# Two groups of outputs inside the recurrence, paired softmax sums, and narrow probabilities in spare blocks: a change to a two-layer hybrid decoder on one core

## The chip, the cores and the metric

The kernel runs on one core of a Trainium2 chip. The metric is the device time of one execution in microseconds (us); lower is better. In the profile, PE is the matrix engine (TensorE) and PEld its weight loads, DVE is VectorE, ACT is ScalarE, POOL is GpSimd and SP is the engine whose queue issues most transfers.

## The reference

Two layers with 512 tokens and a model width of 1024, all in float32. Each layer is a mixer and a gated feed-forward block; a last RMSNorm follows. What matters here is the mixer:

```python
p = n @ w_in                                   # n = RMSNorm(h)
# part A, RWKV-7: 8 heads x 64, per token
sa    = einsum('bhij,bhj->bhi', state, a_t)
state = state * w_t + sa[..., None] * b_t + v_t[..., None] * k_t
y_t   = einsum('bhij,bhj->bhi', state, r_t)
y     = group_norm(y) * lnx_w + lnx_b          # per head, over 64
y_a   = ((y + bonus) * gate) @ w_out_rwkv
# part B, MLA: 8 heads, causal softmax over 512 keys
s = (qn @ k_nope.T + qr @ k_pe.T) * scale;  s = where(key <= query, s, -1e30)
o = softmax(s) @ v
y_b = o @ w_out_mla
h = h + (sigmoid(gate_a) * y_a + sigmoid(gate_b) * y_b) @ w_out
```

## The kernel before

Each large product is three matmuls (`mm3`, lines 254 to 256): weights and operands are split into a high and a low part, and hi x hi, lo x hi and hi x lo are added in one accumulator of PSUM, tile `acc`. Weights stream from memory, 1024 columns at a time, through the queue of SP; ACT makes the high part (line 204) and DVE the low part (line 205).

PSUM has eight banks, and the pools fill all of them. In the second half of the mixer these are two banks `sc`, two banks held as one tile `xy`, one `pt`, one `po`, and two accumulators.

The recurrence is computed in eight chunks of 64 tokens. The loop `for c in range(8)` does, per chunk: eight matmuls of the state with `AR` (line 824), an add on DVE that makes `xs` (line 831), eight matmuls with the inverted triangle in `AM` (line 839), two copies into `Z` by DVE and ACT (line 844), eight matmuls with `BT` (line 849), and an add on DVE that makes the next state `St` (line 857), for which POOL has scaled the old one (line 856). All of these matmuls use parts of the matrix engine (64 x 64 or 128 x 64). So that PE has work while it waits for DVE and ACT, `filler(n)` puts n steps of gate projections between them; a step is one `mm3`. There are 20 steps in the list `rest`. A call of `filler` on an empty list does nothing.

The outputs of the recurrence come two chunks at a time from `chunk_out(i)`, i = 0 to 3. It takes the matmuls of `AR` with the stored states (line 879; half as many at i = 0, where chunk 0 has no state), those of `AM` with `Z` (line 889), then sums over each head on DVE (line 894, into `mu`) and a copy into `Z` by ACT (line 896). All four calls stand behind the recurrence (`outputs`), and use `xy`, of which there is one. `norms` then makes the group norms (lines 904 to 913), and `transposed` turns them (`yop`, line 919) into the operands `yops` of the product with `w_out_rwkv`.

Attention takes two heads at a time: `heads(p)`, p = 0 to 3. It projects keys and queries (three and twelve matmuls), and for each block b of 128 queries and each of the two heads hh it takes scores into an `sc` bank (line 981), scales and masks them and finds the minimum of the negated scores (line 984), exponentiates with the sum as a by-product (line 987), inverts the sum (line 988), scales (line 989), turns the blocks into `pt` (line 992) and copies them into `PT` (line 993). Sixteen matmuls per pair of heads make the output `po` (line 1000).

The program's order on PE is written by hand for the recurrence (`manual_schedule`). Everything else is ordered by a planner, which works through the program by priority in the order of the text and may put later work, such as attention, between the handwritten steps. On DVE, ACT and POOL the planner orders everything. Each engine then runs its list strictly in order.

In the profile each f32 matmul of the source outside `mm3` stands as two records, so the eight matmuls of line 849 are "x16".

Of the kernel before, what the change touches and what calls it, by code (L numbers as in the profile page):

```python
# [9 lines left out]
F32 = mybir.dt.float32  # L10
F32R = mybir.dt.float32r
I32 = mybir.dt.int32
AF = mybir.ActivationFunctionType
# [147 lines left out]
def build(ctx, tc, x, pos, wst, vecd, constd, out):  # L161
# [273 lines left out]
    def mixer(l, ops, nrm, wks):  # L435
        with ExitStack() as mx:
# [244 lines left out]
            def xyt():  # L681
                return pb.tile([128, 2, 512], F32, name="xy", tag="xy")

            with pool(name=f"ti{l}", bufs=2) as ti, tc.manual_schedule(engines={PE.engine}):
# [119 lines left out]
                parts4[6].go(2)  # L804


                St = [None]
                rest = iter([parts4[6]] * 4 + [parts4[7]] * 8 + [parts4[8]] * 8)

                def filler(n):  # L810
                    for _ in range(n):
                        part = next(rest, None)
                        if part:
                            part.go(1)

                for c in range(8):
                    i, e = divmod(c, 2)
                    xy = xyt()
                    if c:
                        for p in (0, 2, 1, 3):  # L820
                            for hh in range(2):
                                k0 = 64 * hh
                                s, ur, vr = slot(c, p)
                                PE.matmul(xy[ur:ur + 64, hh, 64 * p:64 * p + 64], AR[p][k0:k0 + 64, s, ur:ur + 64],
                                          St[c][k0:k0 + 64, p, :], start=True, stop=True, tile_position=(k0, ur))
                        filler(3)
                    us = tl.tile([128, 8, 64], F32, name="xs", bufs=1)
                    for g in range(2):
                        s, ur, vr = slot(c, 2 * g)
                        if c:  # L830
                            V.tensor_tensor(us[ur:ur + 64, 4 * g:4 * g + 4].rearrange("p (q h) i -> p q h i", h=2),
                                            xy[ur:ur + 64, :, 128 * g:128 * g + 128].rearrange("p h (q i) -> p q h i", i=64),
                                            Z[ur:ur + 64, i, e, 256 * g:256 * g + 256].rearrange("p (q h i) -> p q h i", h=2, i=64),
                                            ALU.add)
                    for hd in (0, 4, 1, 5, 2, 6, 3, 7):
                        s, ur, vr = slot(c, hd // 2)
                        g, n = divmod(hd, 4)
                        x = us[ur:ur + 64, hd, :] if c else Z[ur:ur + 64, i, e, 64 * hd:64 * hd + 64]
                        PE.matmul(xy[ur:ur + 64, g, 256 + 64 * n:320 + 64 * n], AM[ur:ur + 64, hd, s, ur:ur + 64], x,  # L839
                                  start=True, stop=True, tile_position=(ur, ur))  # L840
                    filler(2)
                    for g in range(2):
                        s, ur, vr = slot(c, 2 * g)
                        (A.copy if g else V.tensor_copy)(Z[ur:ur + 64, i, e, 256 * g:256 * g + 256], xy[ur:ur + 64, g, 256:512])
                    if c < 7:
                        for p in range(4):
                            for hh in range(2):
                                hd = 2 * p + hh
                                PE.matmul(xy[64 * hh:64 * hh + 64, 0, 64 * p:64 * p + 64], BT[p][:, slot(c, p)[0], 64 * hh:64 * hh + 64],
                                          Z[:, i, e, 64 * hd:64 * hd + 64], start=True, stop=True, tile_position=(0, 64 * hh))  # L850
                        filler(2)
                        Sn = tl.tile([128, 4, 64], F32, name="St", tag="St", bufs=7)
                        ps = xy[:, 0, 0:256].rearrange("p (q i) -> p q i", i=64)
                        if c:
                            tmp = tl.tile([128, 4, 64], F32, name="tmp", tag="tmp", bufs=1)
                            G.tensor_tensor(tmp, St[c], PC[:, c, :, None].to_broadcast([128, 4, 64]), ALU.mult)
                            V.tensor_tensor(Sn, ps, tmp, ALU.add)
                        else:
                            V.tensor_copy(Sn, ps)
                        St.append(Sn)  # L860

            with pool(name=f"tb{l}", bufs=2) as tb:
                def MT(name, tag, bufs=3):
# [1 line left out]

                qops = [split(xp, lat[i], vc(l, "q_norm", i), "xa", 8) for i in range(2)]
                kvop = split(xp, lat[2], None, "xa", 8)


                def chunk_out(i):  # L870
                    xy = xyt()
                    begun, left = set(), {(r, hh): 4 for r in (0, 64) for hh in range(2)}
                    for p in range(4):
                        for e, hh in ((0, 0), (1, 1), (0, 1), (1, 0)):
                            c = 2 * i + e
                            s, ur, vr = slot(c, p)
                            k0 = 64 * hh
                            if c:
                                PE.matmul(xy[vr:vr + 64, hh, 64 * p:64 * p + 64], AR[p][k0:k0 + 64, s, vr:vr + 64],
                                          St[c][k0:k0 + 64, p, :], start=(vr, hh) not in begun, stop=False,  # L880
                                          tile_position=(k0, vr))
                                begun.add((vr, hh))
                    for hh in range(2):
                        for p in range(4):
                            for e in range(2):
                                s, ur, vr = slot(2 * i + e, p)
                                hd = 2 * p + hh
                                left[vr, hh] -= 1
                                PE.matmul(xy[vr:vr + 64, hh, 64 * p:64 * p + 64], AM[:, hd, s, vr:vr + 64],  # L889
                                          Z[:, i, e, 64 * hd:64 * hd + 64], start=(vr, hh) not in begun,  # L890
                                          stop=left[vr, hh] == 0, tile_position=(0, vr))
                                begun.add((vr, hh))
                    mu = tb.tile([128, 16], F32, name="mu", bufs=4)
                    V.tensor_reduce(mu[:, 0:8].rearrange("p (q h) -> p h q", h=2),
                                    xy[:, :, 0:256].rearrange("p h (q i) -> p h q i", i=64), mybir.AxisListType.X, ALU.add)
                    A.copy(Z[:, i, 0, :].rearrange("p (q h i) -> p q h i", h=2, i=64),
                           xy[:, :, 0:256].rearrange("p h (q i) -> p q h i", i=64))
                    return mu


                def group_norm(i, mu):
# [28 lines left out]
                    V.tensor_tensor(bl, bl, gt, ALU.mult)  # L930
                    yops.append(split(xp, bl, None, "xa", 8))

                sums = []

                def outputs():
                    for i in range(4):
                        sums.append(chunk_out(i))

                def norms():
                    for i, gr in enumerate([group_norm(i, sums[i]) for i in range(4)]):  # L940
# [18 lines left out]
                def heads(p):  # L959
# [16 lines left out]
                    PTs = [tb.tile([128, 13, 128], F32, name="PT", tag="PT", bufs=4) for _ in range(2)]  # L976
                    for b in range(4):
                        n = 128 * (b + 1)
                        for hh in range(2):
                            sp = sc()  # L980
                            PE.matmul(sp[:, 0:n], qs[hh][:, 128 * b:128 * b + 128], ks[hh][:, 0:n], start=True, stop=True)  # L981
                            P = MT("P", "P")
                            mn = tb.tile([128, 4], F32, name="mn", bufs=4)
                            V.tensor_tensor_reduce(out=P[:, 0:n], in0=sp[:, 0:n],  # L984
                                                   in1=cst[:, C_CAUS + 512 - n:C_CAUS + 512], scale=-ATT_SCALE,
                                                   scalar=1e30, op0=ALU.add, op1=ALU.min, accum_out=mn[:, 0:1])
                            A.activation(P[:, 0:n], P[:, 0:n], AF.Exp, bias=mn[:, 0:1], scale=-1.0, accum_out=mn[:, 1:2])  # L987
                            V.reciprocal(mn[:, 2:3], mn[:, 1:2])
                            V.tensor_scalar(P[:, 0:n], P[:, 0:n], mn[:, 2:3], None, ALU.mult)
                            pt = pb.tile([128, 512], F32, name="pt", tag="pt")  # L990
                            for kb in range(b + 1):
                                PE.transpose(pt[:, 128 * kb:128 * kb + 128], P[:, 128 * kb:128 * kb + 128], ident)  # L992
                            A.copy(PTs[hh][:, b:4 * b + 1:3, :],  # L993
                                                                 pt[:, 0:n].rearrange("p (k q) -> p k q", q=128))
# [166 lines left out]
```

## Time and profile before

| | |
|---|---|
| three runs | 1543.62, 1544.17, 1545.25 us |
| median | 1544.17 us |
| the profiled execution: its own time | 1545.89 us |
| the profiled execution: span | 1544.1 us |
| granted clock of PE, mean | 0.998 |
| PE busy | 1525.8 us, 99% |
| DVE busy | 919.1 us, 60% |
| ACT busy | 648.2 us, 42% |

The span goes from the first to the last instruction; the execution's own time also has what lies around it, 1.8 us here. A row of the timeline gives the start, the time until the engine has finished, the engine, the source line, what is written and read, and how many instructions are merged into the row; in brackets stands idle time of the engine before it and what ended it. Matmuls overlap, so the distance between two starts says more than the length.

### The profile page before, as it was taken

The numbers are of one execution on the slowest core, as the hardware profiler recorded it, in microseconds if no ns is written. First come the engines' busy times: TensorE is split into PE (matmuls) and PEld (weight loads), VectorE is DVE, ScalarE is ACT, GpSimd is POOL, SyncE is SP. The second block draws the span as 40 slices with busy tenths as digits, with TensorE's granted clock in tenths as the row PEclk, the third lists the DMA queues.
The fourth block names the chain that finished last, engine by engine and source line by source line (L and its number), as shares of the span: only waits on it lengthen the run. The fifth ranks groups of instructions, "written<-read, shape, count | busy, mean of one in ns | idle before, by whom it ended". The sixth has DMA issues, their size and how long they took to land.

```text
span 1544.1 us, 22127 instructions
## 1 busy us (share of the span) xinstructions
PE 1525.8 (99%) x8860; PEld 1230.5 (80%) x8860; DVE 919.1 (60%) x1532; ACT 648.2 (42%) x986; POOL 186.9 (12%) x157
## 2 busy tenths in 40 slices
PE   8999999999999999999999999999999999999998
PEld 6887886678888888888887888766788888888887
DVE  5679886867455555533347668769664555554233
ACT  5545454744443333322235544457344333333222
POOL 0111101300211111100011121013012111111000
PEclk9999999999999999999999999999999999999999
DMA  5424322335332222233334333223352332333232
GB/s 197 136 89 136 112 82 90 97 103 164 109 97 100 97 96 96 96 110 116 116 117 131 101 110 103 77 92 102 111 163 96 96 96 96 98 100 100 98 96 82
DMA packets 57415, 166.05 MB, mean 108 GB/s; under 512 B 6624, under 2 KB 7904, under 8 KB 57312
## 3 DMA queue, kind: packets, MB, share of 16 engines
q1 hardware_dynamic: 57168, 164.64, 32.7%
q8 instruction: 69, 1.13, 0.3%
q14 instruction: 34, 0.28, 0.1%
q10 hardware_dynamic: 144, 0.00, 0.0%
HBM read 147.32 MB, written 17.30 MB: 107 GB/s over the span
## 4 chain that ended last, share of the span: by engine, by line
PE 96%; DVE 2%; issue 1%; ACT 1%; DMA 0%; POOLq 0%; DVEq 0%; ACTq 0%
PE acc L254 28%; PE acc L255 27%; PE acc L256 27%; PE sc L981 2%; PE pt L992 1%; PE po L1000 1%; PE m L616 1%; PE m L254 1%; PE m L256 1%; PE m L255 1%; PE xy L839 1%; PE xy L889 1%; PE xy L734 1%; PE m L624 1%; PE m L521 0%
## 5 line engine op out<-in xcount | busy, mean ns | idle before, releaser
L254 PE MATMUL acc<-hi,whi 128*128 128x512 f32 (+1 forms) x1886 | 741.6, 393 | 6.2 <-ACT hi L290 5.3
L256 PE MATMUL acc<-hi,wlo 128*128 128x512 f32 (+1 forms) x1886 | 735.7, 390 | 0.0
L255 PE MATMUL acc<-lo,whi 128*128 128x512 f32 (+1 forms) x1886 | 734.6, 390 | 0.0
L204 ACT CAST whi<-raw 128x1024 fp32r<-128x1024 f32 (+1 forms) x247 | 253.0, 1026 | 523.6 <-PE acc L255 447.2
L254 PEld LDWEIGHTS acc<-hi,whi 128*128 128x128 f32 x1886 | 355.3, 188 | 79.0 <-ACT hi L290 5.3
L256 PEld LDWEIGHTS acc<-hi,wlo 128*128 128x128 f32 x1886 | 355.0, 188 | 72.8 <-issue 1.0
L205 DVE TENSOR_TENSOR wlo<-raw,whi 128x1024 fp32r<-128x1024 f32 (+1 forms) x247 | 302.0, 1225 | 184.7 <-ACT whi L204 184.2
L255 PEld LDWEIGHTS acc<-lo,whi 128*128 128x128 f32 x1886 | 355.2, 188 | 70.1 <-issue 1.1
L1081 POOL TENSOR_TENSOR c<-c,rstd 128x512 f32<-128x512 f32 x44 | 58.0, 1317 | 403.6 <-ACT c L1080 403.6
L1074 DVE TENSOR_TENSOR u<-acc,rstd 128x512 f32<-128x512 f32 x44 | 30.5, 692 | 104.6 <-PE acc L256 104.4
L1083 DVE TENSOR_TENSOR c<-c,acc 128x512 f32<-128x512 f32 x44 | 30.3, 688 | 86.6 <-POOL c L1081 86.6
L1080 ACT ACTIVATE c<-c 128x512 f32<-128x512 f32 x44 | 27.8, 632 | 81.7 <-DVE c L1079 81.7
L313 POOL TENSOR_TENSOR nv<-nv,cst 128x4 f32<-128x4 f32 (+1 forms) x10 | 11.8, 1180 | 342.6 <-DVE nv L312 342.6
L349 POOL TENSOR_TENSOR nacc<-nacc,nsq 128x512 f32<-128x512 f32 x14 | 24.9, 1779 | 190.3 <-ACT nsq L348 190.3
L981 PE MATMUL sc<-K,q 128*128 128x128 f32 (+3 forms) x128 | 44.1, 444 | 0.2
L987 ACT ACTIVATE P<-P,mn 128x128 f32<-128x128 f32 (+3 forms) x64 | 35.8, 560 | 5.4 <-DVE mn L984 5.1
L1077 ACT ACTIVATE c<-u,vec 128x512 f32<-128x512 f32 x44 | 35.7, 811 | 2.8 <-DVE u L1073 2.8
L468 DVE TENSOR_TENSOR cur<-acc,rstd 128x512 f32<-128x512 f32 x26 | 17.9, 688 | 30.9 <-PE acc L256 25.1
L993 ACT COPY PT<-pt 128x128 f32<-128x128 f32 (+3 forms) x64 | 27.1, 423 | 16.6 <-PE pt L992 16.0
L1079 DVE SCALAR_TENSOR_TENSOR c<-u,vec,c 128x512 f32<-128x512 f32 x44 | 33.1, 752 | 1.5
L1078 DVE SCALAR_TENSOR_TENSOR c<-u,vec,c 128x512 f32<-128x512 f32 x44 | 32.8, 746 | 1.8 <-ACT c L1077 1.8
L992 PEld LDWEIGHTS pt<-cst,P 128*128 128x128 f32 x160 | 18.7, 140 | 15.5 <-ACT PT L993 9.7
(243 smaller groups left out, 1377.8 us busy)
## 6 DMA issues: line engine op xcount, KB each, us to landing
raw<-in_w SPq DMA_DIRECT2D x236, 512.0 KB, 3.3
gate_d<-gg SPq DMA_DIRECT2D x32, 256.0 KB, 2.1
AM<-gate_d SPq DMA_DIRECT2D x16, 256.0 KB, 4.6
gb<-gate_d SPq DMA_DIRECT2D x16, 256.0 KB, 2.8
raw<-in_w SPq DMA_DIRECT2D x8, 256.0 KB, 4.1
h<-in_x SPq DMA_DIRECT2D x8, 256.0 KB, 4.9
rgate_d<-gt SPq DMA_DIRECT2D x8, 256.0 KB, 3.1
bl_d<-rk SPq DMA_DIRECT2D x8, 256.0 KB, 4.3
```

Source lines behind the costliest of these rows:

```text
L204: A.copy(hi, r)
L205: V.tensor_tensor(lo, r, hi.bitcast(F32), ALU.subtract)
L254: PE.matmul(ps, w[0], xx[0], start=first, stop=False)
L255: PE.matmul(ps, w[0], xx[1], start=False, stop=False)
L256: PE.matmul(ps, w[1], xx[0], start=False, stop=last)
L981: PE.matmul(sp[:, 0:n], qs[hh][:, 128 * b:128 * b + 128], ks[hh][:, 0:n], start=True, stop=True)
L987: A.activation(P[:, 0:n], P[:, 0:n], AF.Exp, bias=mn[:, 0:1], scale=-1.0, accum_out=mn[:, 1:2])
L992: PE.transpose(pt[:, 128 * kb:128 * kb + 128], P[:, 128 * kb:128 * kb + 128], ident)
L1077: A.activation(cc, u[:, 2:514], AF.Identity, bias=vc(l, "conv_b", i), scale=vc(l, "conv_w", 2 * FT + i))
L1078: V.scalar_tensor_tensor(cc, u[:, 1:513], vc(l, "conv_w", FT + i), cc, ALU.mult, ALU.add)
L1079: V.scalar_tensor_tensor(cc, u[:, 0:512], vc(l, "conv_w", i), cc, ALU.mult, ALU.add)
L1081: G.tensor_tensor(cc, cc, rstd, ALU.mult)
```

## The change

Three edits, with what they bring along:

1. `chunk_out` moves in front of the recurrence and takes its two PSUM banks as an argument. The calls for i = 0 and 1 stand inside the recurrence, at the end of chunks 3 and 5, and use the two `sc` banks; the calls for 2 and 3 stay behind it, on `xy`. As the halves are now two tiles, sums and copy become two instructions each of half the width. The second `filler(2)` is not called in chunks 3 and 5.
2. In `heads`, the two heads of a block share one tile `mn`: both are exponentiated first, then one `reciprocal` inverts both sums, then each head is scaled and turned.
3. For b = 0 and 1, `P` is written into blocks 7, 10 and 11 of the pair's own `PT` tile, which nothing else uses, and no longer takes one of the three `P` buffers. In the last pair, for odd b, the two heads' turned blocks go into the two halves of an `xy` tile and not one after the other into `pt`.

```diff
+                def chunk_out(i, xy):
...
+                    mu = tl.tile([128, 16], F32, name="mu", bufs=4)
...
+                    for hh in range(2):
+                        ps = xy[hh][:, 0:256].rearrange("p (q i) -> p q i", i=64)
+                        V.tensor_reduce(mus[:, hh, :], ps, mybir.AxisListType.X, ALU.add)
+                        A.copy(Y[:, hh], ps)
+                    sums.append(mu)
...
-                        filler(2)
+                        if c not in (3, 5):
+                            filler(2)
...
                         St.append(Sn)
+                    if c in (3, 5):
+                        chunk_out(c // 2 - 1, [sc(), sc()])
...
-                def chunk_out(i):
-                    xy = xyt()
...
-                    mu = tb.tile([128, 16], F32, name="mu", bufs=4)
-                    V.tensor_reduce(mu[:, 0:8].rearrange("p (q h) -> p h q", h=2),
-                                    xy[:, :, 0:256].rearrange("p h (q i) -> p h q i", i=64), mybir.AxisListType.X, ALU.add)
-                    A.copy(Z[:, i, 0, :].rearrange("p (q h i) -> p q h i", h=2, i=64),
-                           xy[:, :, 0:256].rearrange("p h (q i) -> p q h i", i=64))
...
                 def outputs():
-                    for i in range(4):
-                        sums.append(chunk_out(i))
+                    for i in range(2, 4):
+                        xy = xyt()
+                        chunk_out(i, [xy[:, 0, :], xy[:, 1, :]])
...
                     for b in range(4):
                         n = 128 * (b + 1)
+                        xy3 = xyt() if p == 3 and b % 2 else None
+                        Ps = []
+                        mn = tb.tile([128, 8], F32, name="mn", bufs=2)
                         for hh in range(2):
...
-                            P = MT("P", "P")
-                            mn = tb.tile([128, 4], F32, name="mn", bufs=4)
+                            P = MT("P", "P") if b > 1 else \
+                                PTs[hh][:, 7 + 3 * b:8 + 4 * b, :].rearrange("p k q -> p (k q)")
...
-                            V.reciprocal(mn[:, 2:3], mn[:, 1:2])
-                            V.tensor_scalar(P[:, 0:n], P[:, 0:n], mn[:, 2:3], None, ALU.mult)
-                            pt = pb.tile([128, 512], F32, name="pt", tag="pt")
+                            Ps.append(P)
+                        V.reciprocal(mn[:, 4:6], mn[:, 2:4])
+                        for hh, P in enumerate(Ps):
+                            V.tensor_scalar(P[:, 0:n], P[:, 0:n], mn[:, 4 + hh:5 + hh], None, ALU.mult)
+                            pt = xy3[:, hh, :] if xy3 is not None else pb.tile([128, 512], F32, name="pt", tag="pt")
```

More of the change, by code (lines that the diff above doesn't have):

```diff
@@ L804, in mixer @@
                 parts4[6].go(2)
+                sums = []
+                def chunk_out(i, xy):
+                    begun, left = set(), {(r, hh): 4 for r in (0, 64) for hh in range(2)}
+                    for p in range(4):
+                        for e, hh in ((0, 0), (1, 1), (0, 1), (1, 0)):
+                            c = 2 * i + e
+                            s, ur, vr = slot(c, p)
+                            k0 = 64 * hh
+                            if c:
+                                PE.matmul(xy[hh][vr:vr + 64, 64 * p:64 * p + 64], AR[p][k0:k0 + 64, s, vr:vr + 64],
+                                          St[c][k0:k0 + 64, p, :], start=(vr, hh) not in begun, stop=False,
+                                          tile_position=(k0, vr))
+                                begun.add((vr, hh))
+                    for hh in range(2):
+                        for p in range(4):
+                            for e in range(2):
+                                s, ur, vr = slot(2 * i + e, p)
+                                hd = 2 * p + hh
+                                left[vr, hh] -= 1
+                                PE.matmul(xy[hh][vr:vr + 64, 64 * p:64 * p + 64], AM[:, hd, s, vr:vr + 64],
+                                          Z[:, i, e, 64 * hd:64 * hd + 64], start=(vr, hh) not in begun,
+                                          stop=left[vr, hh] == 0, tile_position=(0, vr))
+                                begun.add((vr, hh))
+                    mu = tl.tile([128, 16], F32, name="mu", bufs=4)
+                    mus = mu[:, 0:8].rearrange("p (q h) -> p h q", h=2)
+                    Y = Z[:, i, 0, :].rearrange("p (q h i) -> p h q i", h=2, i=64)
+                    for hh in range(2):
+                        ps = xy[hh][:, 0:256].rearrange("p (q i) -> p q i", i=64)
+                        V.tensor_reduce(mus[:, hh, :], ps, mybir.AxisListType.X, ALU.add)
+                        A.copy(Y[:, hh], ps)
+                    sums.append(mu)
                 St = [None]
@@ L867, in mixer @@
                 kvop = split(xp, lat[2], None, "xa", 8)
-                def chunk_out(i):
-                    xy = xyt()
[L872 to L892, printed above, removed]
-                    mu = tb.tile([128, 16], F32, name="mu", bufs=4)
-                    V.tensor_reduce(mu[:, 0:8].rearrange("p (q h) -> p h q", h=2),
-                                    xy[:, :, 0:256].rearrange("p h (q i) -> p h q i", i=64), mybir.AxisListType.X, ALU.add)
-                    A.copy(Z[:, i, 0, :].rearrange("p (q h i) -> p q h i", h=2, i=64),
-                           xy[:, :, 0:256].rearrange("p h (q i) -> p q h i", i=64))
-                    return mu
                 def group_norm(i, mu):
@@ L931, in yop @@
                     yops.append(split(xp, bl, None, "xa", 8))
-                sums = []
                 def outputs():
-                    for i in range(4):
-                        sums.append(chunk_out(i))
+                    for i in range(2, 4):
+                        xy = xyt()
+                        chunk_out(i, [xy[:, 0, :], xy[:, 1, :]])
                 def norms():
@@ L981, in heads @@
                             PE.matmul(sp[:, 0:n], qs[hh][:, 128 * b:128 * b + 128], ks[hh][:, 0:n], start=True, stop=True)
-                            P = MT("P", "P")
-                            mn = tb.tile([128, 4], F32, name="mn", bufs=4)
+                            P = MT("P", "P") if b > 1 else \
+                                PTs[hh][:, 7 + 3 * b:8 + 4 * b, :].rearrange("p k q -> p (k q)")
                             V.tensor_tensor_reduce(out=P[:, 0:n], in0=sp[:, 0:n],
                                                    in1=cst[:, C_CAUS + 512 - n:C_CAUS + 512], scale=-ATT_SCALE,
-                                                   scalar=1e30, op0=ALU.add, op1=ALU.min, accum_out=mn[:, 0:1])
-                            A.activation(P[:, 0:n], P[:, 0:n], AF.Exp, bias=mn[:, 0:1], scale=-1.0, accum_out=mn[:, 1:2])
-                            V.reciprocal(mn[:, 2:3], mn[:, 1:2])
-                            V.tensor_scalar(P[:, 0:n], P[:, 0:n], mn[:, 2:3], None, ALU.mult)
-                            pt = pb.tile([128, 512], F32, name="pt", tag="pt")
+                                                   scalar=1e30, op0=ALU.add, op1=ALU.min, accum_out=mn[:, hh:hh + 1])
+                            A.activation(P[:, 0:n], P[:, 0:n], AF.Exp, bias=mn[:, hh:hh + 1], scale=-1.0,
+                                         accum_out=mn[:, 2 + hh:3 + hh])
+                            Ps.append(P)
[3 more added lines that the diff above has]
+                            pt = xy3[:, hh, :] if xy3 is not None else pb.tile([128, 512], F32, name="pt", tag="pt")
                             for kb in range(b + 1):
```

## The prediction

> **What bounds the kernel now.** I read the page first: the share of each engine and the chain that ended last.
>
> ```profile
> PE 1525.8 (99%) x8860; PEld 1230.5 (80%) x8860; DVE 919.1 (60%) x1532; ACT 648.2 (42%) x986; POOL 186.9 (12%) x157
> PE 96%; DVE 2%; issue 1%; ACT 1%; DMA 0%; POOLq 0%; DVEq 0%; ACTq 0%
> ```
>
> PE is busy for 1525.8 of 1544.1 us and is 96% of the chain, so 18.3 us is all that better filling can bring in the whole kernel. The change removes no matmul. Next come the waits of PE, longest first (who waited for whom, total, times, longest).
>
> ```profile
> PE acc L254 <- ACT hi L290: 5.3, 1, 5.3
> PE xy L824 <- DVE St L857: 1.3, 2, 0.6
> PE xy L839 <- DVE xs L831: 1.1, 2, 0.6
> PE acc L254 <- ACT whi L204: 0.9, 1, 0.9
> PE m L624 <- DVE AM L619: 0.8, 2, 0.4
> PE m L559 <- ACT sq L555: 0.7, 1, 0.7
> PE xy L889 <- issue: 0.4, 1, 0.4
> PE xy L919 <- DVE bl L927: 0.2, 1, 0.2
> ```
>
> The first is the start of the kernel, the fourth stands between the layers, and L624 and L559 come before the recurrence: the change reaches none of these. It reaches L824 and L839 (the recurrence, once in each layer), L889 and L919: 3.0 us in all. Then the timeline of PE, to see where in the recurrence the two waits lie (layer 0; layer 1 has the same two with the same lengths).
>
> ```profile
> 245.34 0.39 PE L254 MATMUL acc<-hi,whi 128*128 128x512 f32 x1
> 245.57 0.40 PE L255 MATMUL acc<-lo,whi 128*128 128x512 f32 x1
> 245.80 0.40 PE L256 MATMUL acc<-hi,wlo 128*128 128x512 f32 x1
> 246.13 0.68 PE L839 MATMUL xy<-xs,AM 64*64 64x64 f32 x16
> ...
> 248.33 0.69 PE L849 MATMUL xy<-Z,BT 128*64 128x64 f32 x16
> 249.64 0.46 PE L824 MATMUL xy<-St,AR 64*64 64x64 f32 x16 [0.63 <-DVE St L857]
> 250.03 0.50 PE L955 MATMUL acc<-whi,hi 128*128 128x512 f32 x1
> 251.10 0.68 PE L839 MATMUL xy<-xs,AM 64*64 64x64 f32 x16 [0.57 <-DVE xs L831]
> ...
> 253.45 0.40 PE L255 MATMUL acc<-lo,whi 128*128 128x512 f32 x1
> 253.78 0.69 PE L849 MATMUL xy<-Z,BT 128*64 128x64 f32 x16
> 254.40 0.50 PE L256 MATMUL acc<-hi,wlo 128*128 128x512 f32 x1
> 254.73 0.39 PE L254 MATMUL acc<-hi,whi 128*128 128x512 f32 x1
> ...
> 259.73 0.69 PE L849 MATMUL xy<-Z,BT 128*64 128x64 f32 x16
> 260.34 0.49 PE L981 MATMUL sc<-K,q 128*128 128x128 f32 x2
> ...
> 261.92 0.29 PE L824 MATMUL xy<-St,AR 64*64 64x64 f32 x4
> ```
>
> Counting the L849 rows from the first, 248.33 ends chunk 3 and 259.73 chunk 5. Behind chunk 3 there is nothing to run until the new state is there, 0.63 us; then one L955 runs, and PE idles again, 0.57 us. Behind chunk 5 other work covers the same wait: from 260.34 to 261.92 it is scores (L981) and key and query products.
>
> The list `rest` has 20 steps. Chunk 0 takes 4, chunks 1 and 2 take 7 each, and chunk 3's first call takes the last 2: the six matmuls that end at 245.80. So the `filler(2)` that the change drops in chunks 3 and 5 was empty: that edit costs nothing and brings nothing.
>
> **Edit 1, two outputs inside the recurrence.** Today the first calls stand here:
>
> ```profile
> 270.83 0.47 PE L879 MATMUL xy<-St,AR 64*64 64x64 f32 x16
> 271.24 1.15 PE L889 MATMUL xy<-Z,AM 128*64 128x64 f32 x32
> 272.32 0.55 PE L992 MATMUL pt<-cst,P 128*128 128x128 f32 x3
> ...
> 274.12 0.69 PE L879 MATMUL xy<-St,AR 64*64 64x64 f32 x32
> 274.75 1.15 PE L889 MATMUL xy<-Z,AM 128*64 128x64 f32 x32
> 275.83 0.66 PE L992 MATMUL pt<-cst,P 128*128 128x128 f32 x4
> ```
>
> Group 0 takes 272.32 - 270.83 = 1.49 us of PE, group 1 275.83 - 274.12 = 1.71. That time moves; it does not vanish. Terms, for both layers together:
>
> (a) The wait behind chunk 3 (1.3 in the list of waits, 2 x 0.63). Group 0 needs states 0 and 1 and Z of chunks 0 and 1, long done, so it can run at once, and 1.49 us is more than the 0.7 us between the end of L849's issue (248.33 + 0.62, as at 253.78 to 254.40) and L824. Gone: -1.25 us. What is late next is `xs`, term (b).
>
> (b) The wait for `xs` (2 x 0.57). It has two L831 on DVE ahead of it, and the planner had one L955 to put there, since both accumulators waited for copies. With 1.5 us more ahead, those are free, and three L955 (0.7 us) are ready. In the same slot of chunk 5 the planner put five matmuls and PE waited for nothing. Against it: DVE now has two head sums to do just then. The first can run under the second half of L889; the second starts when L889 ends and takes about as long as the add of L857, and L824 (0.39 us from start to the next, 249.64 to 250.03) covers most of that.
>
> ```profile
> L894 DVE TENSOR_REDUCE mu<-xy 128x8 f32<-128x512 f32 x8 | 5.5, 683 | 0.3 <-PE xy L889 0.3
> L857 DVE TENSOR_TENSOR St<-xy,tmp 128x256 f32<-128x256 f32 x12 | 5.1, 424 | 10.1 <-PE xy L849 8.5 <-ACT Vt L956 1.5
> L896 ACT COPY Z<-xy 128x512 f32<-128x512 f32 x8 | 4.7, 587 | 6.4 <-DVE mu L894 6.2
> L993 ACT COPY PT<-pt 128x256 f32<-128x256 f32 x16 | 5.9, 367 | 5.1 <-PE pt L992 4.9
> ```
>
> Bounds: 0 (or +0.85, if one 424 ns sum sits in front of `xs` in each layer) to -1.13. I take -1.1, as the slot of chunk 5 is the nearest row.
>
> (c) Borders. Wide matmuls start 0.23 us apart (245.34 to 245.57); the last before a block of small ones takes 0.33 (253.45 to 253.78), and so does the first behind it (254.40 to 254.73): 0.20 us for an excursion. Four moved groups lose theirs, as small blocks then stand side by side: -0.8 us; bounds 0 (the planner makes as many elsewhere) and -1.2 (the work that now sits behind chunk 5 joins other wide work, 2 x 0.2 more). [...]
>
> (d) DVE and ACT. All eight `chunk_out` split: DVE 16 x 0.424 - 8 x 0.683 = +1.3 us, ACT 16 x 0.367 - 8 x 0.587 = +1.2 us. Neither lies on the path, apart from what (b) counts. No transfer moves, and no queue of SP or POOL is passed.
>
> (e) What fill is missing later. 3.2 us of PE work in each layer is now done earlier, and 1.2 us of it into holes. It stood where attention of the first heads waits on DVE and ACT, which are nearly full there:
>
> ```profile
> 271.00:284.00 13.00, 12.97 (x281) 10.03 (x277) 10.10 (x26) 8.13 (x18) 6.31 (x6) 1.00 0.49 165
> 284.00:298.00 14.00, 13.93 (x70) 9.16 (x70) 13.29 (x48) 11.91 (x33) 6.92 (x6) 1.00 0.14 42
> ```
>
> (Columns: length, busy PE, PEld, DVE, ACT, POOL.) DVE has 13.29 of 14 us. Where fill lacked in chunk 4, a hole was 0.6 us. I estimate one such hole in each layer: +1.2; bounds 0 and +2.4 (two each). Also, the scores need the `sc` banks that groups 0 and 1 hold; group 1 wants both while scores at 260.34 have one. If that costs, it is this same kind of hole.
>
> **Edit 2, one inversion for a pair.**
>
> ```profile
> L988 DVE RECIPROCAL mn<-mn 128x1 f32<-128x1 f32 x64 | 9.8, 156 | 3.2 <-ACT P L987 3.1
> L987 ACT ACTIVATE P<-P,mn 128x128 f32<-128x128 f32 (+3 forms) x64 | 35.8, 560 | 5.4 <-DVE mn L984 5.1
> L987 ACT ACTIVATION_READ_ACCUMULATOR P<-P,mn 128x1 f32 x64 | 12.1, 189 | 0.0
> ```
>
> 32 x 0.156 = 5.0 us less on DVE, which is off the path: 0. It adds a wait: the first head's scaling waits for the second head's exponential, 0.56 + 0.19 = 0.75 us, and the first head's turns on PE and the copy of ACT stand behind it. Work of key and query products and of `yops` covers it as long as there is any: 0, bound +0.75 for each uncovered pair (rival 2).
>
> **Edit 3, spare blocks and a second bank for turned blocks.** No PE wait for a `P` buffer or for `pt` is in the list, so 0; in the last pair two excursions a layer may merge (4 x 0.2 = 0.8 us at best, in the range only). The waits at L889 (0.43) and L919 (0.2) may go or stay: taken as 0.
>
> **The sum.** -1.25 - 1.1 - 0.8 + 1.2 = -1.95, about -2.0 us. Against the profiled execution: span 1544.1 and 1.8 around it, 1545.89, which is 1.72 above the median of the three runs; it becomes 1543.9, and the median 1544.17 becomes 1542.2, or 0.13% less. About 0.2% (3.1 us) is what a measurement of this kernel can tell from no change.
>
> **The rivals.** 1. Everything closes: (a), (b), (c), no new hole, and the L889 and L919 waits (0.6) go too, with a little from merged turns: -1.25 - 1.1 - 0.8 - 0.6 - 0.3 = -4.05, 1540.1 us. For it: the list of waits shows only these in the stage, and DVE gets 5.0 us of room. Against it: DVE at 13.29 of 14 us leaves the planner's guesses little slack.
>
> 2. Slower: the pair's wait takes the place of the one removed. Place: the first two pairs of heads, before the first `yops` product, when PE has only key and query products to run. Price: eight blocks a layer, 0.75 us each; with half of them uncovered, 3.0 us a layer, 6.0 in all, against -3.15 won: +2.85, 1547.0 us. It decides from about 4 uncovered blocks of 16 on (3.15 / 0.75). For it: 3.2 us of fill has left just this stretch. Against it: before, PE waits here for no exponential at all, and the planner may swap in other work.
>
> 3. The holes only move: a list in fixed order with all its work gets the same idle time elsewhere, 1544.2 us (between 1543.3 and 1545). For it: PE's matmuls are the same, and the removed fillers were empty. Against it: the hole behind chunk 3 is directly covered by work that needs nothing.
>
> **How the numbers follow.** Forecast 0.41, rival 1 0.25, rival 3 0.22, rival 2 0.12. The predicted time is that of the forecast, 1542.2 us. The range takes in rivals 1 and 3 with their spread, and leaves out rival 2 and the far ends: 1539.2 to 1545.4; the forecast's own is 1541.1 to 1543.3. Faster by over 0.2% (below 1541.1): rival 1 and the forecast's edge, 0.27. Within 0.2%: 0.63. Slower by over 0.2% (above 1547.3): half of rival 2, and what I can't name, 0.10.
>
> **What would show it.** (a) L879 and L889 right behind L849 of chunk 3, and no bracket at the L824 that follows. (b) At least three L955 between L824 and L839 of chunk 4, and no bracket. (c) Fewer changes between L879 or L889 and L992 after the recurrence. (e) and rival 2: brackets on PE with L987, L988 or L989 as the releaser between the end of the recurrence and the first yops product. PE's idle total of 18.3 us should come to some 17. The prediction is wrong if L824 or L839 of chunks 4 to 7 still wait for L857 or L831, or if the group at chunk 5 waits for `sc`.

## The result and the profile after

The changed kernel takes 0.9987 of the time before, with a 95% interval of 0.9981 to 0.9993: medians 1543.19 and 1545.29 us over 22 runs each, 2.1 us less. The profiled execution has 1543.04 us, 2.85 less than the one before, at a span of 1541.3 us.

Who PE waited for, after (total, times, longest; the lines of `chunk_out` are now 817 to 837, AR in the recurrence 857, AM 872, BT 882, the new state 891, scores 988, turns 1002, their copy 1003):

```profile
PE acc L254 <- ACT hi L290: 5.4, 1, 5.4
PE acc L254 <- ACT whi L204: 0.9, 1, 0.9
PE m L624 <- DVE AM L619: 0.8, 2, 0.4
PE m L559 <- ACT sq L555: 0.6, 1, 0.6
PE pt L1002 <- ACT PT L1003: 0.5, 2, 0.2
PE sc L988 <- ACT Z L837: 0.3, 2, 0.2
PE acc L959 <- ACT Vt L960: 0.3, 2, 0.2
```

The waits for `St` (1.3) and `xs` (1.1) are gone; three of 0.2 each time are new. The timeline of PE shows why (layer 0, chunk 3 into chunk 4, then chunk 5 into 6):

```profile
249.51 0.69 PE L882 MATMUL xy<-Z,BT 128*64 128x64 f32 x16
250.13 0.47 PE L817 MATMUL sc<-St,AR 64*64 64x64 f32 x16
250.53 1.15 PE L827 MATMUL sc<-Z,AM 128*64 128x64 f32 x32
251.61 0.46 PE L857 MATMUL xy<-St,AR 64*64 64x64 f32 x16
252.00 0.50 PE L959 MATMUL acc<-whi,hi 128*128 128x512 f32 x1
...
253.13 0.50 PE L959 MATMUL acc<-whi,hi 128*128 128x512 f32 x1 [0.16 <-ACT Vt L960]
253.57 0.68 PE L872 MATMUL xy<-xs,AM 64*64 64x64 f32 x16
...
261.49 0.69 PE L882 MATMUL xy<-Z,BT 128*64 128x64 f32 x16
262.11 0.70 PE L817 MATMUL sc<-St,AR 64*64 64x64 f32 x32
262.73 1.15 PE L827 MATMUL sc<-Z,AM 128*64 128x64 f32 x32
263.82 0.46 PE L857 MATMUL xy<-St,AR 64*64 64x64 f32 x16
264.45 0.46 PE L988 MATMUL sc<-K,q 128*128 128x128 f32 x2 [0.17 <-ACT Z L837]
```

Both groups stand directly behind BT, and no L857 waits for its state. The columns of DVE and ACT at the same place show what is late next:

```profile
250.34 0.42 DVE L891 TENSOR_TENSOR St<-xy,tmp 128x256 f32<-128x256 f32 x1 [0.75 <-PE xy L882]
251.27 0.92 DVE L836 TENSOR_REDUCE mu<-sc 128x4 f32<-128x256 f32 x2 [0.50 <-PE sc L827]
252.22 0.88 DVE L864 TENSOR_TENSOR xs<-xy,Z 64x256 f32<-64x256 f32 x2
```

```profile
251.73 0.86 ACT L837 COPY Z<-sc 128x256 f32<-128x256 f32 x2 [1.90 <-DVE mu L836]
252.49 1.11 ACT L960 COPY Vt<-acc 128x512 f32<-128x512 f32 x2
```

The state is ready at 250.76, long before L857. The two head sums end just as `xs` can start. But the two copies of group 0 stand ahead of the `Vt` copies on ACT, and the fourth value product needs an accumulator that a `Vt` copy frees: 0.16 us.

**A measure that does not swing.** Single executions differ by more than 3 us (1541.8 to 1545.67), for reasons of which one is told at the end. So I read the stage in which the change acts on PE, from the layer's first 32 x 32 matmul (L784) to the next column sums in `stat` (L333). Before, layer 0:

```profile
217.95 0.24 PE L784 MATMUL sc<-T,AM 32*32 32x32 f32 x3
...
416.60 0.28 PE L333 MATMUL stat<-cst,nacc 128*128 128x1 f32 x2
```

That is 198.65 us. After, layer 0:

```profile
219.12 0.57 PE L784 MATMUL sc<-T,AM 32*32 32x32 f32 x24
...
416.74 0.50 PE L333 MATMUL stat<-cst,nacc 128*128 128x1 f32 x4
```

That is 197.62: -1.03 us. Layer 1 goes from 198.87 to 197.65, -1.22; -2.25 us together, or -2.06 by twice layer 0. The 198.87 has 0.43 us in it for which the profile shows nothing that PE waits for, the "issue" wait at L889. I call such a wait instruction supply: in all five stages that have one, PE goes on 1.2 to 1.4 us after the end of a transfer of the kind "instruction", of which the kernel has 69 on one queue. That this transfer is the cause is suggested by it, not shown. A second profile of the changed kernel, from a later session, gave 197.60 and 197.65. "Changes of kind" below is the number of times, in the first 125 us of the stage, that PE goes from one kind of matmul to another (wide accumulation, scores, turns, heads' output, small recurrence blocks, 64 x 64 and 128 x 64 apart): 151 in a layer before, 140 after.

| kernel | stage, layer 0 | layer 1 | changes of kind | time against before |
|---|---|---|---|---|
| before | 198.65 | 198.87 (i) | 151 | |
| edits 1, 2 and 3 | 197.62 | 197.65 | 140 | 0.9987 [0.9981, 0.9993] |
| the same again | 197.60 | 197.65 | 140 | 0.9984 [0.9975, 0.9993] |
| 1 | 197.79 | 197.78 | 147 | 0.9983 [0.9974, 0.9992] |
| 3 | 198.40 | 198.49 | 141 | one run |
| 2 and 3 | 198.54 | 198.48 | 137 | 1.0000 [0.9990, 1.0009] |
| 1 and 2 | 202.01 | 202.01 | 144 | one run |
| 1 and 3 | 196.76 | 197.66 (i) | 136 | 0.9986 [0.9977, 0.9995] |
| 1 and 3 again | 196.70 | 196.85 | 136 | 0.9981 [0.9972, 0.9990] |
| 1 and 3 without the second bank | 196.71 | 196.88 | 136 | one run |
| 1 with group 0 alone | 199.82 | 201.25 (i, c) | 143 | one run |
| the same with 2 and 3 | 199.62 | 200.52 (i) | 146 | one run |
| 1 with three groups | 202.68 (i) | 203.74 (c) | 135 | one run |
| before, filler spread otherwise | 202.37 (c) | 201.32 | 141 | 1.0033 [1.0020, 1.0045] |

(i): 0.4 to 0.9 us of instruction supply falls into it. (c): 3.41 us at half the clock (granted clock 0.50) fall into it; one such stretch cost 1.54 us where it could be read (last section).

### The profile page after: what moved, and what is told of

It reads as the page before. It is cut to its first block, busy times and chain, and to the rows that moved or that the text cites. A ratio compares the mean times of both kernels' runs of the same rounds, so it can differ in the third digit from the quotient of the medians.

```text
span 1541.3 us, 22081 instructions
## 1 busy us (share of the span) xinstructions
PE 1524.9 (99%) x8860; PEld 1229.9 (80%) x8860; DVE 917.1 (60%) x1508; ACT 649.1 (42%) x994; POOL 184.7 (12%) x157
## 4 chain that ended last, share of the span: by engine, by line
PE 94%; DVE 3%; ACT 1%; issue 1%; DMA 0%; POOL 0%; POOLq 0%; DVEq 0%; ACTq 0%
PE acc L254 28%; PE acc L256 27%; PE acc L255 27%; PE sc L988 1%; PE po L1010 1%; PE pt L1002 1%; PE m L616 1%; PE m L254 1%; PE m L256 1%; PE m L255 1%; PE xy L872 1%; PE xy L734 1%; PE xy L882 1%; PE m L624 1%; PE m L521 0%
## 5 line engine op out<-in xcount | busy, mean ns | idle before, releaser
L988 PE MATMUL sc<-K,q 128*128 128x128 f32 (+3 forms) x128 | 43.9, 440 | 0.4 <-ACT Z L837 0.3
L288 DVE TENSOR_TENSOR lo<-c,hi 128x512 fp32r<-128x512 f32 x44 | 30.1, 685 | 1.4 <-ACT hi L287 1.4
L287 ACT CAST hi<-c 128x512 fp32r<-128x512 f32 x44 | 27.4, 622 | 8.5 <-DVE c L1093 6.1
L554 POOL TENSOR_TENSOR n<-n,cst 128x8 f32<-128x8 f32 x8 | 18.5, 2309 | 96.2 <-DVE n L553 96.2
```

## The experiments

**Edit 1 alone.** The change with `heads` as before.

```diff
-                        V.reciprocal(mn[:, 4:6], mn[:, 2:4])
-                        for hh, P in enumerate(Ps):
...
+                            V.reciprocal(mn[:, 2:3], mn[:, 1:2])
```

`P` again takes one of the three buffers in every block, and the turned blocks go into `pt` alone.

> Edit 1 alone: groups 0 and 1 inside the recurrence, softmax sums and P as before. The stage is read on PE from its first 32x32 matmul of a layer (line 784) to the next column sums in stat (line 333): 198.65 and 198.87 us before, 197.62 and 197.65 after the whole change, so -2.25 us for both layers. Theory (the holes behind chunk 3 are covered and four excursions of PE saved): this kernel has nearly all of it, -1.7 to -2.3 us in the two stages, no idle at the matmuls of AR in chunk 4, execution 0.10 to 0.15% shorter. Rival A (the room on DVE that the paired inversions make is what counts): at most -0.8 us here. Rival B (the holes only move): the old idle is gone, other idle of the same size stands after the recurrence, 0 +- 0.4 us.

-0.86 and -1.09 us, -1.95 in all (-1.72 by twice layer 0), as the theory had it; 1542.76 us against 1545.41. No wait at L857; of the waits for `xs`, 0.27 us is left in each layer, at L872 of chunk 7. The room that paired inversions make on DVE is not what counts.

**Edits 2 and 3 alone.** The kernel before, with the new `heads`.

> Edits 2 and 3 alone: paired inversions, P of narrow blocks in PT, the second bank in the last pair; all outputs behind the recurrence as before. Theory: 0 +- 0.5 us in the two stages against 198.65 and 198.87, both holes of chunk 4 still there (0.63 and 0.57 us in each layer), execution within 0.05%. Rival A: -1.5 us or more. The slower rival of the prediction (a pair's wait uncovered): +0.75 us for each uncovered pair, and brackets on PE with the exponential or the scaling as releaser.

-0.11 and -0.39, time unchanged. Of its waits of PE, the two old ones and the largest new one:

```profile
PE xy L824 <- DVE St L857: 1.3, 2, 0.6
PE xy L839 <- DVE xs L831: 1.1, 2, 0.6
PE pt L998 <- DVE P L995: 1.0, 2, 0.5
```

L998 is the turn and L995 the scaling: the bracket that rival 2 named, once in each layer, 0.5 us. PE makes 14 changes of kind fewer, and idles 0.4 us longer in layer 0. That the two balance here was not in the prediction, which put both at nothing, each with a bound.

**Group 0 alone inside.**

```diff
-                    if c in (3, 5):
-                        chunk_out(c // 2 - 1, [sc(), sc()])
+                    if c == 3:
+                        chunk_out(0, [sc(), sc()])
```

> Edit 1 with group 0 alone moved, behind chunk 3; groups 1 to 3 stay behind the recurrence, softmax as before. Theory: the holes of chunk 4 are group 0's, so this has -1.25 (the state) and some -0.8 (xs) of both layers and half of the saved excursions: -1.6 to -2.0 us in the two stages, and what group 1 adds is at most -0.5. Rival (each group brings the same, as it is excursions that count): -1.1 us, half of the whole. Rival B (holes move): 0 +- 0.4.

All three were wrong: +1.17 us in layer 0. The holes of chunk 4 are closed just as in the whole change, but a larger one opens 35 us later. PE, then DVE:

```profile
283.82 0.81 PE L985 MATMUL sc<-K,q 128*128 128x384 f32 x2
286.44 0.91 PE L985 MATMUL sc<-K,q 128*128 128x384 f32 x2 [1.81 <-DVE mn L988]
```

```profile
283.65 0.42 DVE L836 TENSOR_REDUCE mu<-xy 128x4 f32<-128x256 f32 x1 [0.44 <-ACT Z L837]
284.52 1.52 DVE L909 SCALAR_TENSOR_TENSOR Z<-mu,Z 128x512 f32<-128x512 f32 x1 [0.44 <-ACT Z L837]
285.97 0.41 DVE L988 CUSTOM_DVE_ANT_0 P<-sc,cst 128x256 f32<-128x256 f32 x1
```

The minimum L988 would free a score bank for PE. In DVE's list it stands behind a group norm (L909), which waits for the copy of ACT. PE has nothing else next in its own list. PE stops at 284.63, when L909 has just begun, and goes on when L988 is done. The late copy holds L909 back by 0.44 us; the larger part is that L909 takes 1.52 us, where the same operation mostly takes 0.69 (last section). So in a list of fixed order one slow operation stopped PE for 1.8 us.

**The same with edits 2 and 3.**

> The whole change, but group 1 stays behind the recurrence: group 0 alone inside, edits 2 and 3 in. Moving group 0 alone without edits 2 and 3 gave a new hole of 1.8 us in each layer: a score on PE waits for a minimum on DVE that the planner put behind head sums and a group norm. Theory A (that hole is an accident of the fixed orders): with other orders around it, it is gone or under 0.5 us, and the two stages take -1.0 to -2.3 us against 198.65 and 198.87. Theory B (with three groups behind the recurrence and their fill gone, PE has too little to run there): a hole of over 1 us in each layer again, the stages +1 us or longer.

+0.97 us in layer 0, with 2.07 us of idle: 0.49 at a turn behind a scaling, 0.56 at a turn behind a copy, 0.39 at `yop` behind POOL, and three of about 0.2. Neither theory as it stood: the one hole of 1.8 us is gone, as A says, but others take its place and the stage is longer, as B says. That too little is left to run there was not separated from a poor order. So it stays open why group 0 alone loses a microsecond and both groups win one.

**The hole filled with other work.** No edit of the change; the 20 filler steps are dealt out so that two land behind BT of chunk 3.

```diff
-                        filler(3)
+                        filler(2)
...
-                    filler(2)
+                    if c != 3:
+                        filler(2)
```

The first of these calls stands behind AR, the second between AM and BT.

> No edit of the change. The kernel before, with its 20 filler steps dealt out otherwise: two in place of three behind the AR matmuls, none between AM and BT of chunk 3, so that two are left behind the BT matmuls of chunk 3, where the change puts group 0. Theory (any work that is ready closes those holes): the idle at AR of chunk 4 goes, and most of that at xs; -1.2 to -2.2 us in the two stages, without the change. Rival (it has to be the outputs, because of the excursions they save): -0.5 us at most. Rival B: a new hole at xs of chunks 1 to 3, where a step less is left: 0 or longer than before.

1.0033 of the time before: rival B. The theory was right about the place: behind BT of chunk 3 the two steps cover the wait for the state in chunk 4, and no L824 waits there. But other waits come. In layer 0, PE waits 0.72 us for `xs` in chunk 1, which the third step had covered, and 1.30 us in chunk 4, now at BT. PE, then DVE:

```profile
251.12 0.68 PE L839 MATMUL xy<-xs,AM 64*64 64x64 f32 x16
253.11 0.69 PE L850 MATMUL xy<-Z,BT 128*64 128x64 f32 x16 [1.30 <-ACT Z L845]
```

```profile
250.99 1.21 DVE L205 TENSOR_TENSOR wlo<-raw,whi 128x1024 fp32r<-128x1024 f32 x1
252.23 0.43 DVE L845 COPY Z<-xy 64x256 f32<-64x256 f32 x1
```

AM is through at 251.80, but the copy behind it on DVE waits for the low part of a weight, 1.21 us. So the filler steps that were moved were no spare work: one of them had covered a wait, and the new order has another wait besides. Groups 0 and 1 together could be moved at a smaller price; group 0 alone could not.

**Three groups inside.**

```diff
-                    if c in (3, 5):
+                    if c in (3, 5, 7):
```

> Edit 1 carried on: groups 0, 1 and 2 inside the recurrence (behind chunks 3, 5 and 7), group 3 behind it; softmax as before. Theory A: what counts is the two holes of chunk 4, already closed by group 0; -1.5 to -2.2 us in the two stages, as with two groups (-1.95). Theory B (each moved group saves excursions): -2.3 to -2.8. Theory C (scores wait longer for the sc banks): 0.3 us or more of idle at the scores in each layer, where it was 0.17, and -1.5 us or less.

All theories missed: +4.03 us in layer 0, 0.73 of it instruction supply, though PE makes only 135 changes of kind. The first scores of layer 0, and then its waits (totals of both layers):

```profile
274.50 0.71 PE L985 MATMUL sc<-K,q 128*128 128x128 f32 x4
```

```profile
PE sc L985 <- DVE mn L988: 2.4, 5, 1.3
PE xy L872 <- DVE xs L864: 2.0, 2, 1.0
PE xy L857 <- DVE St L891: 1.2, 2, 0.6
PE xy L882 <- ACT Z L877: 1.0, 2, 0.5
```

The scores start ten us later than in the whole change (264.45), behind the group that takes both `sc` banks last. Chunks 6 and 7 have nothing else to put between their steps, and the `St` wait of 0.6 us that the change closes at chunk 4 is back at chunk 7. Theory C had a cause that the rows show, the scores' wait for `sc`, but not the size, nor the waits of the recurrence itself (4.2 of the 6.6 us listed) that follow when the scores are not there to fill it.

**Edits 1 and 3 without the pairing.**

```diff
-                        V.reciprocal(mn[:, 4:6], mn[:, 2:4])
-                        for hh, P in enumerate(Ps):
-                            V.tensor_scalar(P[:, 0:n], P[:, 0:n], mn[:, 4 + hh:5 + hh], None, ALU.mult)
+                            V.reciprocal(mn[:, 2:3], mn[:, 1:2])
+                            V.tensor_scalar(P[:, 0:n], P[:, 0:n], mn[:, 2:3], None, ALU.mult)
```

> Edits 1 and 3 without edit 2: outputs inside the recurrence, P of narrow blocks in PT, the second bank in the last pair, but each head inverts its own sum. Edit 1 alone took -1.95 us off the two stages, the whole change -2.25. Theory A (the paired inversion costs a wait of the first head, and what is won comes from edit 3): -2.3 to -2.9 here, better than both. Theory B (the pairing lets PE do both heads' turns in one go, which saves changes between kinds of matmul: 140 in a layer with the whole change, 147 with edit 1 alone): -1.8 to -2.1 here, and 145 or more changes. Execution 0.1 to 0.2% shorter than before either way.

-1.89 us in layer 0; layer 1 has 0.70 us of instruction supply, and -1.21 with it. Theory A, with -3.10 for both a little more than its range, and B falls: there are 136 changes of kind, fewer than with the pairing. So the saved changes come from edit 3, and the pairing costs 0.9 us a layer. In layer 0, 0.4 of this is idle time of PE (0.5 us without the pairing, 0.9 with it); the rest was traced to no wait.

**Edits 1 and 2 without edit 3.** `P = MT("P", "P")` for every block, and `xy3 = None`.

> Edits 1 and 2 without edit 3: outputs inside, paired inversions, P always in its own three buffers, turned blocks always into pt. Theory A (edit 3 is what the pairing needs, as a pair holds two P buffers of three at a time): idle at scores or turns grows, and the stages are at -1.9 us or less. Theory B (edit 3 is off the path): -2.0 to -2.4, as the whole change.

Theory A, and far beyond its bound: +3.36 us in layer 0. The wait of DVE that carries it, from 255 to 335 us: here, in the whole change, with edit 1 alone, and before.

```profile
DVE P L990 <- PE pt L1001: 6.5, 7, 2.4
```

```profile
DVE P L991 <- PE pt L1002: 0.7, 2, 0.4
```

```profile
DVE P L988 <- PE pt L996: 0.9, 3, 0.4
```

```profile
DVE P L984 <- PE pt L992: 0.3, 1, 0.3
```

With edits 1 and 3 without the pairing there is no such wait.

With the pairing two of three `P` buffers are held until both heads are scaled and turned. DVE then stands 6.5 us for a buffer, all it has behind that waits too, and PE waits for scores' minima, turns and copies. Writing narrow `P` into spare blocks of `PT` is what makes the pairing bearable; the second bank, which this kernel lacks as well, brings nothing without the pairing (below), and was not tested apart with it.

**Edit 3 alone.** The kernel before with `P` of narrow blocks in `PT` and the second bank.

> Edit 3 alone, on the kernel before: P of narrow blocks in PT and the second bank in the last pair; each head inverts its own sum, all outputs behind the recurrence. Theory A (edit 3 is worth some 0.8 us a layer by itself, through fewer changes between kinds of matmul): the two stages take -1.0 to -1.8 us against 198.65 and 198.87, both holes of chunk 4 still there. Theory B (it pays only with the outputs inside): 0 +- 0.5.

-0.25 and -0.38 us: nearer to theory B, whose 0.5 for both layers it passes by a little. It saves ten changes of kind, and a new wait gives most of it back: L879 of group 3 waits 0.66 us in each layer for the copy of ACT that frees `xy` from group 2.

```profile
PE xy L879 <- ACT Z L896: 1.3, 2, 0.7
```

With groups 0 and 1 inside, two groups and not four pass through `xy`, no such wait is in the list, and the same edit brings -1.0.

**Edit 3 without the second bank.** Edits 1 and 3 with `xy3 = None`.

> Edit 1 and the first half of edit 3: P of narrow blocks in PT, but turned blocks always into pt, no second bank in the last pair; no pairing. With the second bank the stages took 196.76 and 197.66 us (the second with 0.70 of instruction supply in it), with neither half 197.79 and 197.78. Theory A (the freed P buffers are it): as with both, 196.6 to 197.0 in a layer without that disturbance. Theory B (the merged turns of the last pair are it): 197.5 or longer.

196.71 and 196.88 us, as with it: theory A. The second bank for the last pair's turns brings nothing that can be read.

**Without the pairing, and whole, on one chip.** Both kernels again.

> Edits 1 and 3 without the pairing, a second time, on one chip with the whole change. Theory (the pairing costs a wait in this kernel): the stages take 196.7 to 197.0 us where nothing disturbs them, 0.6 to 0.9 less than the whole change in each layer, and the execution is 0.05 to 0.15% shorter than that of the whole change. Rival: the two agree within 0.05%.

> The whole change again, beside the kernel without the pairing on the same chip. Expected: the stages take 197.6 us each, the execution 0.10 to 0.19% less than before.

The stages came as expected: 196.70 and 196.85 without the pairing, 197.60 and 197.65 whole, 0.90 and 0.80 us less a layer. The times did not tell them apart, as the rival had it: medians 1542.32 and 1542.51 us (11 runs each), 0.01% apart, ratios 0.9981 [0.9972, 0.9990] and 0.9984 [0.9975, 0.9993]. Over all runs of this study the medians are 1542.2 (22 runs) and 1543.0 (33), a difference of half of what the two stages say. By the stages, edits 1 and 3 are the better version; by the times that is not shown, nor that edits 2 and 3 add anything to edit 1 (0.9983).

## Why the prediction was right, point by point

The forecast was 0.13% less, and 0.13% was measured. The waits that it said would go are gone: no AR or AM matmul of chunks 4 to 7 waits for its state or for `xs`, group 1 does not wait for `sc`, and PE's idle total went from 18.3 to 16.4 us, where some 17 was forecast. That the sum fits so well is in part luck: (b) and (c) each brought about 0.3 us less than forecast, and (e) cost about 0.6 less. The terms:

- (a) The wait behind chunk 3, -1.25: right. Both are gone, wherever group 0 stands there.
- (b) The wait for `xs`, -1.1: 0.16 us remains of 0.57, so -0.8 for both layers. The step that was mis-sized left ACT out of it. The bound on DVE was right (a 128x256 head sum takes 425 ns, and `xs` starts 0.03 us behind the second); but the copies of the group precede those of `Vt`.
- (c) Borders, -0.8: idle of PE in the two stages (gaps over 0.03 us) went from 3.41 to 1.68 us, -1.73, with the 0.43 at L889, taken as 0, in it; the stages lost 2.25, so 0.5 is left for borders and all else. That it is the borders is not shown: edit 1 alone saves four changes of kind in a layer and has 0.6, the whole change saves eleven and has 0.5. The small blocks themselves cost the same in both places: L817 and L827 take 0.40 and 1.08 us at the new one (250.13, 250.53, 251.61), L879 and L889 took 0.41 and 1.08 at the old one (270.83, 271.24, 272.32).
- (d) 16 sums of 0.42 and 16 copies of 0.37 us: as costed, and off the path but for the 0.16 us of (b) and the 0.17 us that the scores wait for a copy in (e).
- (e) New holes, +1.2 for both layers: in the whole change they are 0.17 (scores wait for a bank that group 1 holds), 0.13 (L817) and 0.24 (a turn waits for `pt`), less what L919 and its neighbours lost, about +0.3 a layer. Mis-sized by half. "Nearly full" holds for the second of its two windows alone; in the first DVE has 10.10 of 13 us. And the size hangs on the planner's order: 0.8 us of idle in a layer for the whole change, 3.7 without edit 3, 4.6 with three groups.
- Edits 2 and 3 at nothing: the sum holds (-0.15 us a layer from edit 1 alone to the whole change), its parts do not. With edit 1 in, edit 3 brings -1.0 us a layer (197.79 to 196.70, 197.78 to 196.85) and the pairing takes back 0.9. The step that failed is the one that read "no PE wait for a `P` buffer is in the list, so 0". It is DVE that writes `P`, so a wait for its buffers stands in DVE's list: 0.3 us before, 0.9 with edit 1 alone, none once narrow `P` has blocks of its own; and the pairing, which holds two buffers at once, makes it 0.7, or 6.5 without edit 3. Of the -1.0 us, half is idle time of PE; what makes the other half is not shown. The forecast had the right sum here with two wrong terms, by luck, and only runs of the parts show it.
- The terms do not stand alone. (a) and most of (b) are group 0's, and with group 0 alone both waits are gone and the stage is still 1.17 us longer. The sum was right for the two groups together.

Rival 2, the slower one, comes nearest to the kernel of edits 1 and 2, which is slower because of the pairing, but by another mechanism: DVE waits for a `P` buffer that a pair holds. The wait that rival 2 named was seen with edits 2 and 3 alone, once a layer, 0.5 us. Rival 3 is refuted for the whole change, but in several variants the holes did move, and grew.

## What to carry to other kernels

Where an engine is 99% busy and every list has a fixed order, look for work that is ready early and needed late, and put it where that engine waits: group 0 closed the 1.25 us here in every kernel that had it there. But ask what the work leaves behind: filler taken from another place opened waits there, and so did group 0 when it was moved alone. Cost an edit that holds buffers longer against the number of those buffers, and in the waits of the engine that fills them. And measure a gain of a few microseconds between two landmarks of the trace, part by part: two parts of one change were -1.0 and +0.9 us a layer, which its total hides.

## What the runs showed of the hardware

In the middle of the run the granted clock of the matrix engine falls to 0.50 for 3.41 us at a time, and where it does depends on the execution: of the two profiles of the changed kernel, the first has no such stretch (1.00 from 957.60 to 961.00), and the second has one from 957.59 to 961.00. In the kernel with group 0 alone, layer 1, then layer 0 (busy columns PE, PEld, DVE, ACT, POOL; then the granted clock):

```profile
1047.03:1050.44 3.41, 1.60 (x11) 0.67 (x6) 2.80 (x5) 1.81 (x6) 1.94 (x2) 1.00 0.00 0
1050.44:1053.86 3.42, 3.42 (x10) 2.37 (x9) 2.26 (x10) 2.42 (x6) 1.66 (x1) 0.50 0.00 0
```

```profile
282.45:285.86 3.41, 2.18 (x15) 0.94 (x11) 2.53 (x6) 1.23 (x3) 2.71 (x2) 1.00 0.00 0
285.86:289.27 3.41, 2.83 (x11) 1.85 (x12) 3.13 (x12) 2.76 (x7) 0.99 (x1) 1.00 0.01 2
```

The hole is the same 1.81 us in both layers. In layer 1 it lies in the first of the two stretches, with PE busy for 1.60 of 3.41 us, and the clock is 0.50 in the second; in layer 0 the two share it, with 2.18 and 2.83 us busy, and the clock is 1.00 in both. So this hole is not always followed by the lower clock, and what decides it is not shown. Nor does the lower clock come behind idle time alone. In the kernel before:

```profile
954.23:957.64 3.41, 3.41 (x52) 3.11 (x51) 3.24 (x9) 1.35 (x2) 0.00 (x0) 1.00 0.45 154
957.64:961.05 3.41, 3.41 (x10) 2.67 (x9) 3.09 (x7) 2.11 (x4) 1.16 (x1) 0.50 0.38 121
```

PE is busy all through the first, 3.41 of 3.41 us, with wide matmuls, 64 x 64 blocks and column sums one column wide, and the clock is 0.50 in the second. The changed kernel's profiled execution has no such stretch, but its start was slower for longer: its wide matmuls start 0.43 us apart until 11.45, where the one before has this until 8.44, and 0.23 behind it. That is also the distance in the stretch at 0.50 (0.43 from 958.03 to 958.46); the column of the clock reads 1.00 at the start (5.30 to 8.73 before, 8.10 to 11.51 after), so a lower clock there is an estimate from the distances. Aligned by the wide matmuls the changed kernel is 1.29 us late after the start. At 957 it is 0.19 us late, and at 961, behind the slow stretch of the other, 1.35 early: the stretch cost 1.54 us. So of the 2.85 us between the two profiled executions 2.25 lie in the two stages, 0.25 is the balance of these chances (1.54 less 1.29), and the rest was not traced. Nor does the clock explain all of the spread of single executions: of the 22 of the changed kernel, those with a mean clock of 0.999 average 1543.2 us and those with 0.997 1544.6, but those with 0.998 alone go from 1541.8 to 1545.67.

One thing was seen and not tested: L909 took 1.52 us on DVE in the kernel with group 0 alone, where the same operation (line 904) has a mean of 690 ns before; POOL was at work on the same tile for 0.98 of it. The 14 profiles have this operation 112 times. In 98 it takes 0.67 to 0.69 us, and POOL's wide operations (on `Z`, L918 in that kernel, or a copy into `K`) overlap it by at most 0.53 us; in 14 it takes 1.10 to 1.53, and they overlap it by at least 0.55. That they hold DVE up is suggested by this, not tested.
